# Expert stage of a transformer layer: pools that wait tile by tile, a new order of the left-hand pools, and another pace of the gate steps

## The chip, the cores and the metric

The kernel runs on one core of a Trainium2 chip. The metric is the device time of one execution in microseconds (us). Engines are named as in the profile: PE (TensorE; PEld its weight loads), DVE (VectorE), ACT (ScalarE), POOL (GpSimd, which issues the row gathers) and SP (SyncE, which issues nearly all direct DMA transfers). A queue name with a q, such as SPq, means DMA issues.

## The reference

One layer over 1024 tokens of width 1024: modulation, projections, windowed attention with a context of 256 tokens, a short convolution, a merge, and then an expert layer (PEER) whose 16384 experts are single rows of two tables. The expert layer is what this document is about:

```python
def peer(h, w_q, sub_keys, u_tab, v_tab):          # per chunk t of 128 tokens
    qh = (t @ w_q).reshape(T, 8, 2, 128)
    s = jnp.einsum('thpd,hpnd->thpn', qh, sub_keys)         # 128 scores per head and half
    s_top, i_top = lax.top_k(s, 16)
    cand = s_top[:, :, 0, :, None] + s_top[:, :, 1, None, :]
    best, pos = lax.top_k(cand.reshape(T, 8, 256), 16)      # 16 of 256 pairs
    idx = ...                                               # expert numbers, 128 per token
    g = jax.nn.softmax(best, axis=-1)
    act = jax.nn.gelu(jnp.einsum('thkd,td->thk', jnp.take(u_tab, idx, axis=0), t))
    return jnp.einsum('thk,thkd->td', g * act, jnp.take(v_tab, idx, axis=0))
```

The layer's result goes through a last rmsnorm.

## The kernel before

The tokens are two halves of 512. Up to about 1090 us the kernel does everything ahead of the experts; `stage2` of the second half ends with the scores of 16 key chunks, whose top values and their indices go to `sv` and `si`. The selection for the first half (`gates(0)`) runs beside it in the pool "gate0".

In the expert stage the first half is done densely: all 128 blocks of 128 experts are multiplied with all 512 tokens, and a gate matrix, zero for experts not chosen, weights the result. `slot_dense` (L1158) is one block i1. It loads the block of `v` (`v32`, 512 KB), and two slots ahead that of `u`, both in four shared buffers (tag uv32), splits each into two f16 parts (`uh` and `vh` on ACT, `ul` and `vl` on DVE), does 24 `ups` matmuls of 512 columns, a gelu on ACT into `gel`, the product of `gel` with the gates `gt` on DVE, and splits that into `wdh` (ACT) and `wdl` (DVE). Four slots make a group; in the four slots after it the group's eight outputs are done, two in a slot, each 4 x 3 matmuls of 512 columns (`res` for five of them, which stay in PSUM, and `vps` for three, which DVE adds into `part`). For the first three blocks `gel` comes from DRAM, where `early_u` put it; the weights of blocks 3 to 5 (`u_first`) are loaded and split through the pool "wts" before the stage, and that pool is then closed. The second half's tokens are done partly in that way, for 384 tokens (`slot_mix`, no `ups` of its own; its gates are built in the course of the first half), while for 128 tokens of it, and for the dot products of all 512, rows are gathered: `dots` gathers 4 x 128 rows of `u` (POOL) and multiplies each with the token on DVE; `rows_out` does so with `v`.

Gates come in steps. `select` picks the experts of 128 tokens (12 steps, nearly all on DVE; four of them hold the wide `eq` operations; it ends in `ci`, the row numbers that the gathers need). `build_g` spreads them into the gate matrix (20 steps: one-hot products `e`, `ah`, `al` on DVE, 16 `fbank` matmuls of 128 columns on PE, copies into `ge` on ACT, and after two steps a write of `ge` to DRAM (`gd`, 1 MB), from where `gt` is loaded). In the expert stage `ge` has one buffer and its write is issued from ACT's queue. `gates_stream` (L1043) orders selections 0, 1, 2, build 0, selection 3, build 1, build 2; a build waits for the dots of its tokens and yields False until they are done.

`run_side` (L1059) weaves this into the main loop. After each main step it takes as many row steps and gate steps as are due. The gate steps' due count `gdue` grows by 1 in each main step until selection 0 is done, then by GATES_D (L36) times what the main step spent on PE by a meter (columns / 2370); a step that yields False ends the inner loop and leaves `gdue` as it is. What is left when the main loop ends is done at once. The loop runs over 376 main steps (one in each of the first four slots, then three in a slot); row steps come at 478/361 for each. In order of the first half's slots, from slot 8 on (PIN_FROM, L47), PE, DVE and ACT keep the order in which the program was written; before that, and on SP and POOL throughout, a planner of the framework orders the work by its own estimate of when each instruction can start.

A pool is a stretch of SBUF (left-hand or right-hand stack) or of PSUM. Where a new pool takes the place of closed ones, its first tiles wait until everything in the closed pools that lie under it is released. `run` (L1408) closes "gate0", "x1", "s2", "half1", "wts" and two PSUM pools and then opens, one after the other, "psV" (PSUM), "acc" (left), "dense0" (left) and "gate1" (right, in `open_gate`, L1016). From the bottom, the left stack holds "const", and, in the closed part, "wts" (24 KB a partition: four weight tiles `whl`, two `w32`), "half1" (32 KB: `hT`, `cT`, `aT` of the second half) and "gate0".

Of the kernel before, what the change touches and what calls it, by code (L numbers as in the profile page):

```python
# [11 lines left out]
F16 = mybir.dt.float16  # L12
# [6 lines left out]
PSUM = bass.MemoryType.PSUM  # L19

D = 1024
# [10 lines left out]
NDENSE = 512  # L32
NMIX = 384
LATE_DOTS = 34
GATES_B = 0.64
GATES_D = 0.072  # L36
AHEAD = 1
GR = 8
GATE_AT = (2, 5)
# [3 lines left out]
SUB = 4  # L43
# [79 lines left out]
class K:  # L123
# [9 lines left out]
        self.waiting = []  # L133
        self.turned = None

    def pool(self, name, side=None, space=None, bufs=1):
        kw = {}
        if side is not None:
            kw["side"] = side
        if space is not None:  # L140
            kw["space"] = space
        g = self.tc.tile_pool(name=name, bufs=bufs, **kw)
        p = g.__enter__()
        return g, p
# [871 lines left out]
    def open_gate(self, name, side, ge_bufs):  # L1016
        nc, a = self.nc, self.a
        self.ge_bufs = ge_bufs
        g, self.pg = self.pool(name, side=side)
        p = self.pg  # L1020
        io32 = p.tile([128, 128], F32, name="io32", tag="dot", bufs=1)
        nc.sync.dma_start(io32, a["iota"])
        io16 = p.tile([128, 128], F16, name="iotas")
        nc.vector.tensor_copy(io16, io32)
        self.iota = io16.rearrange("p (a b) -> p a b", b=REP).unsqueeze(1).to_broadcast([128, TB, 128 // REP, REP])
        self.cand = p.tile([128, 8, NCAND], F32, name="cand", tag="cand", bufs=1)
        nc.vector.memset(self.cand[:, :, 16:128], NEG)
        self.iota16 = p.tile([128, 16, 16], F16, name="iota16")
        nc.vector.tensor_copy(self.iota16, io32[:, 0:16].unsqueeze(2).to_broadcast([128, 16, 16]))
        return g  # L1030
# [28 lines left out]
    def run_side(self, main, gates=None, grate=0.0, rows=None, rate=0.0, first=None):  # L1059


        pe, dve = self.nc.tensor, self.nc.vector
        last = pe.spent
        due = gdue = 0.0
        alive = gates is not None
        for _ in main:
            spent = pe.spent - last
            with nullcontext() if dve.pin else self.tc.issue_after(dve.last):
                due += rate
                while due >= 1.0:  # L1070
                    due -= 1.0
                    if next(rows, False) is False:
                        due = 0.0
                gdue += 1.0 if first is not None and first not in self.sel else grate * spent
                while alive and gdue >= 1.0:
                    r = next(gates, StopIteration)
                    alive = r is not StopIteration
                    if r is False:
                        break
                    gdue -= 1.0  # L1080
            last = pe.spent
        if alive:
            for _ in gates:
                pass
# [50 lines left out]
    def split_v(self, i1, v32, p):  # L1135
        if v32 is None:
            return self.vparts[i1]
        vh = p.tile([128, D], F16, name="vh", tag="vh", bufs=2 * SUB)
        vl = p.tile([128, D], F16, name="vl", tag="vl", bufs=2 * SUB)
        self.nc.scalar.activation(vh, v32, AF.Copy, scale=16.0)  # L1140
        self.late[0].append((vl, v32, 16.0, vh))
        if i1 >= 128 - 2 * SUB:
            self.vparts[i1] = vh, vl
        return vh, vl
# [13 lines left out]
    def slot_dense(self, i1, p, pv, outs):  # L1158
        nc = self.nc
        nb = NDENSE // 32  # L1160
        hh, hl = self.h2h[0], self.h2l[0]
        self.load_u(i1 + 2, p)
        v32 = self.load_v(0, i1, p)
        self.block_gates(0, i1, p)
        wh = self.pac.tile([128, NDENSE], F16, name="wdh", tag="wdh", bufs=2 * SUB)
        wl = p.tile([128, NDENSE], F16, name="wdl", tag="wdl", bufs=2 * SUB)
        ge = p.tile([128, NDENSE], F32, name="gel", tag="gel", bufs=2)
        if i1 < UPRE:
            nc.sync.dma_start(ge, self.ged[i1])
        else:  # L1170
            uh, ul = self.uparts.pop(i1)
            ps = pv.tile([128, 512], F32, name="ups", tag="v", bufs=3)
            for k in range(8):
                self.mm3(ps, uh[:, k, :], ul[:, k, :], hh[:, k, :], hl[:, k, :], k == 0, k == 7)
        self.lows(1)
        self.lows(0)
        if outs:
            yield 0
        if i1 >= UPRE:
            nc.scalar.activation(ge, ps, AF.Gelu, scale=2.0 ** -12)  # L1180
        self.split_u(i1 + 2, p)
        vh, vl = self.split_v(i1, v32, p)
        ends = []
        for k, out in enumerate(outs):
            ends.append(out())
            if k == 0:
                yield 0
        for end in ends:
            end()
        gev = ge.rearrange("p (b t) -> p b t", t=16)  # L1190
        for q in range(2):
            qs = slice(nb * q, nb * q + nb)
            nc.vector.tensor_mul(gev[:, qs, :], gev[:, qs, :], self.gts[q][:, :, i1 % GR, :])
        nc.scalar.activation(wh, ge, AF.Copy, scale=256.0)
        self.late[0].insert(0, (wl, ge, 256.0, wh))
        yield 0
        return vh, vl, wh, wl

    def slot_mix(self, i1, p, outs):
        nc = self.nc  # L1200
        nb = NMIX // 32
        v32 = self.load_v(1, i1, p)
        self.block_gates(1, i1, p)
        self.lows(0)
        vh, vl = self.split_v(i1, v32, p)
        wh = self.pac.tile([128, NMIX], F16, name="wdh", tag="wdh", bufs=2 * SUB)
        wl = p.tile([128, NMIX], F16, name="wdl", tag="wdl", bufs=2 * SUB)
        parts = [w.rearrange("p (b t) -> p b t", t=16) for w in (wh, wl)]
        for q in range(2):
            qs = slice(nb * q, nb * q + nb)  # L1210
            g = self.gts[q][:, :, i1 % GR, :]
            nc.scalar.activation(parts[0][:, qs, :], g, AF.Copy, scale=256.0)
            self.late[0].insert(q, (parts[1][:, qs, :], g, 256.0, parts[0][:, qs, :]))
        yield 1
        self.lows(0)
        for out in outs:
            out()()
            yield 1
        return vh, vl, wh, wl
# [166 lines left out]
    def experts(self, p, pv):  # L1386
# [4 lines left out]
        steps = 3 * 128 - 2 * SUB  # L1391
        self.run_side(islice(main, steps), self.gates_stream(), GATES_D, rows, (512 - LATE_DOTS) / (steps - 15.0), (1, 0))
        accs[0] = self.whole_acc("acc0")
# [14 lines left out]
    def run(self):  # L1408
# [9 lines left out]
        for hf in (1, 0):  # L1418
            g, p = self.pool(f"half{hf}", side="left")
# [39 lines left out]
        self.close(g_pw)  # L1459
        self.close(g_pa)  # L1460
        self.close(g_pf)
        g_pv, pv = self.pool("psV", space=PSUM)
        self.pf, self.ftag = pv, ("v", 3)
        self.bank = self.fbank
        g_ac, self.pac = self.pool("acc", side="left")
        self.part = self.pac.tile([128, 8 - NRES, HALF], F32, name="part")
        gd, pd = self.pool("dense0", side="left")
        g_g = self.open_gate("gate1", "right", 1)
        self.experts(pd, pv)
        self.close(gd)  # L1470
        self.close(g_ac)
        self.close(g_g)
        self.close(g_pv)
        self.close(self.g_pc)
# [63 lines left out]
```

## Time and profile before

| | |
|---|---|
| median of three runs | 3026.91 us (3026.48 to 3030.73) |
| the profiled execution | 3026.57 us, its span 3024.8 us |
| mean granted TensorE clock | 0.981 |
| PE, DVE, ACT, POOL busy | 95%, 88%, 39%, 35% |
| moved by DMA | 795.74 MB, 263 GB/s over the span |

The numbers of the stretches are times in us from the start of the span. A granted clock of 1.00 is 2.4 GHz, 0.50 is 1.2 GHz. The expert stage begins about 1075 (first `ups`), its first half ends about 2480, and its second half about 3010.

### The profile page before, as it was taken

Reading aid. Unit: us, or ns where it says so; the run is one execution under the profiler, and the core shown is the slowest. Engines: PE = TensorE matmul, PEld = TensorE weight load, DVE = VectorE, ACT = ScalarE, POOL = GpSimd, SP = SyncE. Lnnn points to the kernel's source line nnn. Section 1 sums busy time; section 2 is a strip of 40 time slices with the busy share of each in tenths; the row PEclk is TensorE's granted clock in tenths of the full one; section 3 lists DMA queues with packets and bytes.
Section 4 is the critical chain, followed back from the end, with each engine's and each line's share of the span. In section 5 each row is a group of like instructions: output and inputs, shape, how many; then the busy total and the mean of one; then the engine's idle time right before and its main releaser. Section 6 shows DMA issues by size and latency. Waiting matters only on the chain.

```text
span 3024.8 us, 49092 instructions
## 1 busy us (share of the span) xinstructions
PE 2869.4 (95%) x18685; PEld 1527.1 (50%) x18685; DVE 2647.7 (88%) x5438; ACT 1174.2 (39%) x1878; POOL 1063.1 (35%) x814
## 2 busy tenths in 40 slices
PE   6899999989989978999999999999999989999998
PEld 2465555444444433444444444444444446767675
DVE  7788776699999979999899998999979979888887
ACT  4844576423434232233233332333333323433342
POOL 3200012201121004554444444555444435455553
PEclk9999999999999988999999999999999999999999
DMA  6234436654445448899899998999989989999995
GB/s 225 94 116 123 117 125 183 227 169 151 177 167 192 160 154 287 321 334 321 307 321 345 341 345 292 328 328 333 342 318 334 325 294 316 381 366 351 349 365 197
DMA packets 327197, 795.74 MB, mean 263 GB/s; under 512 B 22960, under 2 KB 147248, under 8 KB 319792
## 3 DMA queue, kind: packets, MB, share of 16 engines
q1 hardware_dynamic: 219536, 372.08, 37.1%
q0 software_dynamic: 103968, 395.36, 35.4%
q10 hardware_dynamic: 3456, 25.17, 2.0%
q8 instruction: 146, 2.39, 0.3%
q14 instruction: 91, 0.75, 0.1%
HBM read 696.31 MB, written 96.21 MB: 262 GB/s over the span
## 4 chain that ended last, share of the span: by engine, by line
PE 44%; DVE 16%; issue 6%; POOL 3%; DMA 3%; ACT 1%; SPq 0%; DVEq 0%; POOLq 0%; ACTq 0%
PE res L72 23%; PE ups L72 13%; PE vps L72 5%; DVE row L72 3%; POOL row L917 3%; DMA row<-u,ci 2%; DVE vl L72 1%; PE fbank L72 1%; DVE e L72 1%; DVE eq L72 1%; PE bank L72 1%; DVE ul L72 1%; DVE si L72 1%; DVE wdl L72 1%; DVE sv L72 1%
## 5 line engine op out<-in xcount | busy, mean ns | idle before, releaser
L917 POOL DMA_INDIRECT row<-u,ci x512 | 674.6, 1318 | 899.5 <-DVE row L72 637.7
L72 DVE SCALAR_TENSOR_TENSOR row<-row,hn 128x1024 f32<-128x1024 f32 x512 | 614.6, 1223 | 75.5 <-DMA row<-u,ci 57.9
L72 PEld LDWEIGHTS <-vh 128*128 128x128 f16 x5120 | 469.6, 98 | 357.3 <-issue 24.3
L72 PE MATMUL res<-wdl,vh 128*128 128x128 f16 (+2 forms) x2176 | 628.2, 306 | 13.7 <-DVE wdl L72 13.6
L72 PE MATMUL res<-wdh,vh 128*128 128x128 f16 (+2 forms) x2176 | 625.6, 306 | 12.2 <-ACT wdh L72 12.2
L72 PE MATMUL res<-wdh,vl 128*128 128x128 f16 (+2 forms) x2176 | 625.3, 306 | 4.7 <-DVE vl L72 4.7
L72 PE MATMUL ups<-h,uh 128*128 128x512 f16 x1952 | 582.4, 380 | 0.0
L72 PEld LDWEIGHTS <-whl 128*128 128x128 f16 x3288 | 317.5, 100 | 370.8 <-issue 50.0
L72 PE MATMUL bank<-hT,whl 128*128 128x512 f16 x1584 | 378.7, 388 | 15.4 <-ACT hT L72 6.0
L72 ACT ACTIVATE vh<-v 128x1024 f16<-128x1024 f32 x248 | 260.1, 1049 | 307.1 <-PE res L72 163.0
L72 PE MATMUL ups<-h,ul 128*128 128x512 f16 x976 | 371.3, 380 | 5.6 <-DVE ul L72 5.6
L72 PEld LDWEIGHTS <-vl 128*128 128x128 f16 x2560 | 250.8, 98 | 195.8 <-DVE vl L72 22.9
L72 DVE SCALAR_TENSOR_TENSOR vl<-v,vh 128x1024 f16<-128x1024 f32 x248 | 301.9, 1218 | 10.3 <-ACT vh L72 10.3
L72 PEld LDWEIGHTS <-uh 128*128 128x128 f16 x1952 | 190.9, 98 | 228.7 <-issue 1.9
L917 POOL DMA_INDIRECT row<-v,ci x128 | 217.3, 1698 | 173.6 <-DVE wdl L72 88.6
L72 ACT ACTIVATE gel<-ups 128x512 f32<-128x512 f32 x125 | 74.6, 597 | 403.1 <-PE ups L72 392.2
L72 ACT ACTIVATE wdh<-gel 128x512 f16<-128x512 f32 x128 | 80.5, 629 | 354.1 <-DVE gel L72 338.0
L72 ACT ACTIVATE ge<-fbank 128x512 f32<-128x512 f32 x224 | 121.6, 594 | 222.3 <-PE fbank L72 187.0
L72 DVE SCALAR_TENSOR_TENSOR racc<-row,fig,racc 128x1024 f32<-128x1024 f32 x127 | 162.6, 1281 | 9.3 <-DMA row<-v,ci 7.0
L72 DVE TENSOR_TENSOR e<-iotas,ii 128x1024 f16<-128x1024 f16 x224 | 153.3, 708 | 7.9 <-ACT ii L72 4.8
L72 PEld LDWEIGHTS <-ul 128*128 128x128 f16 x976 | 95.6, 98 | 122.4 <-DVE ul L72 7.0
L72 PE MATMUL vps<-wdh,vh 128*128 128x512 f16 x384 | 145.6, 379 | 5.2 <-ACT ge L72 4.3
(223 smaller groups left out, 4211.4 us busy)
## 6 DMA issues: line engine op xcount, KB each, us to landing
v<-v SPq DMA_DIRECT2D x248, 512.0 KB
u<-u_t SPq DMA_DIRECT2D x122, 512.0 KB
gd<-ge POOLq DMA_DIRECT2D x32, 1024.0 KB
gt<-gd SPq DMA_DIRECT2D x32, 1024.0 KB
wm<-w_mod SPq DMA_DIRECT2D x48, 512.0 KB
gd<-ge ACTq DMA_DIRECT2D x24, 1024.0 KB
gt<-gd SPq DMA_DIRECT2D x32, 768.0 KB
w<-w_in SPq DMA_DIRECT2D x34, 512.0 KB
```

The source lines that it names most:

```text
L72: r = f(*args, **kw)
L917: self.nc.gpsimd.indirect_dma_start(out=r, out_offset=None, in_=tab, in_offset=bass.IndirectOffsetOnAxis(ap=ci[:, s:s + 1], axis=0))
```

## The change

Five pools, "psV", "acc", "dense0", "gate0" and "gate1" (the last two through `open_gate`), are opened with `reuse_waits="tile"`: a new tile then waits for what lay under that tile alone. A sixth pool of this kind, "parts", is opened on the left below "acc"; the tiles `vh`, `vl` and `wdl` move from "dense0" into it (8 buffers of 2, 2 and 1 KB a partition, 40 KB), so that "acc" (`part`, `wdh`; 14 KB) and the rest of "dense0" (`v32`/`u32`, `gt`, `gel`, `uh`, `ul`) lie 40 KB higher. GATES_D goes from 0.072 to 0.085, and where the gate stream yields False, `gdue` is cut to at most 1.

```diff
-GATES_D = 0.072
+GATES_D = 0.085
@@ pool
-    def pool(self, name, side=None, space=None, bufs=1):
-        kw = {}
+    def pool(self, name, side=None, space=None, bufs=1, **kw):
@@ open_gate
-        g, self.pg = self.pool(name, side=side)
+        g, self.pg = self.pool(name, side=side, reuse_waits="tile")
@@ run_side
                     if r is False:
+                        gdue = min(gdue, 1.0)
                         break
@@ split_v
-        vh = p.tile([128, D], F16, name="vh", tag="vh", bufs=2 * SUB)
-        vl = p.tile([128, D], F16, name="vl", tag="vl", bufs=2 * SUB)
+        vh = self.ppt.tile([128, D], F16, name="vh", tag="vh", bufs=2 * SUB)
+        vl = self.ppt.tile([128, D], F16, name="vl", tag="vl", bufs=2 * SUB)
@@ slot_dense (and slot_mix with NMIX)
-        wl = p.tile([128, NDENSE], F16, name="wdl", tag="wdl", bufs=2 * SUB)
+        wl = self.ppt.tile([128, NDENSE], F16, name="wdl", tag="wdl", bufs=2 * SUB)
@@ run
-        g_pv, pv = self.pool("psV", space=PSUM)
+        g_pv, pv = self.pool("psV", space=PSUM, reuse_waits="tile")
-        g_ac, self.pac = self.pool("acc", side="left")
+        g_pt, self.ppt = self.pool("parts", side="left", reuse_waits="tile")
+        g_ac, self.pac = self.pool("acc", side="left", reuse_waits="tile")
-        gd, pd = self.pool("dense0", side="left")
+        gd, pd = self.pool("dense0", side="left", reuse_waits="tile")
         self.close(g_ac)
+        self.close(g_pt)
```

## Rows read from the trace of the kernel before

**Rows 1.** The page's first part: engine, busy us (share of span), instructions.

```profile
PE 2869.4 (95%) x18685; PEld 1527.1 (50%) x18685; DVE 2647.7 (88%) x5438; ACT 1174.2 (39%) x1878; POOL 1063.1 (35%) x814
```

**Rows 2.** Chain of waits in order of time: start, us, engine, tile, count.

```profile
1543.39 2.59 PE res L72 x12
...
1549.47 5.18 PE ups L72 x24
```

**Rows 3.** Stretches: length; busy PE, PEld, DVE, ACT, POOL; clock; DMA share; GB/s.

```profile
1028.00:1062.00 34.00, 33.25 (x209) 17.15 (x207) 34.00 (x206) 8.00 (x13) 0.00 (x0) 1.00 0.29 94
1062.00:1092.40 30.40, 27.00 (x143) 12.63 (x141) 23.39 (x136) 4.65 (x7) 0.00 (x0) 0.94 0.13 37
1092.40:1104.40 12.00, 0.05 (x2) 0.11 (x2) 2.71 (x9) 1.74 (x3) 0.00 (x0) 0.63 0.97 315
1104.40:1148.00 43.60, 37.12 (x152) 15.34 (x152) 43.60 (x146) 19.87 (x25) 0.55 (x1) 0.89 0.55 180
1148.00:1170.00 22.00, 15.02 (x53) 5.83 (x52) 15.09 (x35) 3.75 (x5) 10.62 (x11) 0.72 1.03 371
```

**Rows 4.** Timeline of SP's DMA issues: start, us, queue, line, transfer.

```profile
1028.25 24.65 SPq L170 DMA_DIRECT2D whl<-ws_wq  x6
1062.01 0.33 SPq L173 DMA_DIRECT2D w<-u_t  x1
...
1092.47 0.33 SPq L1132 DMA_DIRECT2D v<-v  x1
```

**Rows 5.** What SP's queue waited for, 1060 to 1210: us, times, longest.

```profile
SPq L1022 <- DVE si L72: 21.8, 1, 21.8
...
SPq L1132 <- PE ups L72: 7.0, 1, 7.0
```

**Rows 6.** Timeline of POOL, 1000 to 1100: its only instruction.

```profile
1004.93 0.53 POOL L1009 DMA_DIRECT2D gd<-ge  x1 [7.04 <-ACT ge L72]
```

**Rows 7.** Timeline of DVE at the start; in brackets idle before, and releaser.

```profile
1097.26 1.22 DVE L72 SCALAR_TENSOR_TENSOR vl<-v,vh 128x1024 f16<-128x1024 f32 x1 [10.32 <-ACT vh L72]
1102.92 0.76 DVE L72 TENSOR_TENSOR gel<-gel,gt 128x256 f32<-128x256 f32 x2 [4.44 <-DMA gel<-ged]
...
1146.18 0.29 DVE L72 SCALAR_TENSOR_TENSOR ci<-fig 128x128 int32<-128x128 f32 x1
```

**Rows 8.** Stretches with selections, then with a build; columns as in rows 3.

```profile
1180.00:1490.00 310.00, 304.93 (x1403) 137.10 (x1401) 298.35 (x578) 96.77 (x123) 156.53 (x117) 0.99 0.89 317
1512.00:1775.00 263.00, 261.81 (x1402) 126.49 (x1401) 247.87 (x395) 93.35 (x130) 124.39 (x96) 1.00 0.94 337
```

**Rows 9.** Timeline of DVE: one `eq` step, and a slot without a step.

```profile
1404.38 0.68 DVE L72 TENSOR_TENSOR eq<-iota,ab 128x1024 f16<-128x1024 f16 x1
...
1407.54 1.22 DVE L72 SCALAR_TENSOR_TENSOR row<-row,hn 128x1024 f32<-128x1024 f32 x1
...
1562.23 1.22 DVE L72 SCALAR_TENSOR_TENSOR ul<-u,uh 128x1024 f16<-128x1024 f32 x1
...
1571.01 1.21 DVE L72 SCALAR_TENSOR_TENSOR ul<-u,uh 128x1024 f16<-128x1024 f32 x1
```

**Rows 10.** What PE waited for, 1175 to 2455: us, times, longest.

```profile
PE res L72 <- DVE wdl L72: 6.2, 3, 2.9
...
PE res L72 <- DVE vl L72: 3.3, 5, 0.8
```

**Rows 11.** Stretches at the end of the first half; columns as in rows 3.

```profile
2462.90:2478.50 15.60, 7.68 (x82) 6.58 (x81) 11.36 (x18) 4.84 (x10) 1.04 (x1) 0.76 0.65 221
...
2482.00:2999.00 517.00, 515.96 (x4606) 356.85 (x4604) 432.63 (x607) 197.65 (x395) 270.11 (x170) 1.00 0.94 341
```

**Rows 12.** Timeline of ACT at the end of the first half.

```profile
2470.34 2.29 ACT L72 ACTIVATE ge<-fbank 128x512 f32<-128x512 f32 x4 [5.70 <-DMA gd<-ge]
```

More of the change, by code (lines that the diff above doesn't have):

```diff
@@ L1206, in slot_mix @@
         wh = self.pac.tile([128, NMIX], F16, name="wdh", tag="wdh", bufs=2 * SUB)
-        wl = p.tile([128, NMIX], F16, name="wdl", tag="wdl", bufs=2 * SUB)
+        wl = self.ppt.tile([128, NMIX], F16, name="wdl", tag="wdl", bufs=2 * SUB)
         parts = [w.rearrange("p (b t) -> p b t", t=16) for w in (wh, wl)]
```

## Prediction, made before the changed kernel was built

> **What bounds the kernel now.** The page's first part is read first: TensorE (PE) is busy for 95% of the span and DVE for 88% [rows 1]. A share that high says only that a gain must come from time in which PE stands still or runs at its lower clock. The chain of waits in order of time shows the steady state of the expert stage: 24 `ups` matmuls in 5.18 us and each output of 12 matmuls in 2.59 us [rows 2], so 0.216 us a matmul of 512 columns, and a slot of one `ups` and two outputs is 5.18 + 2 x 2.59 = 10.36 us. Then the table of stretches shows where that rate is missed, and there are two places: the start of the stage [rows 3] and the end of its first half [rows 11]. From 2482 to 2999 PE is busy for 516 of 517 us [rows 11], and the diff touches nothing there but where tiles lie.
>
> At the start PE is idle for all of 1092.4 to 1104.4, then has 152 matmuls in 43.6 us and 53 in 22 us, at granted clocks of 0.89 and 0.72 [rows 3]. Together 207 matmuls in 77.6 us; at 0.216 us they need 44.7 us, so 33 us are lost. Why: SP issues the last weight load at 1062.01 and the first `v` load only at 1092.47, with 30 us between in which its queue moves little (DMA share 0.13) [rows 3, 4]. The waits of SP's queue name what held it: the last `si` of the scores for the iota load, and the last `ups` matmul for the first `v` [rows 5]. These are releases of whole pools: `ups` reads weights of the closed pool "wts", and nothing in `v32` needs them. The data were there long before, since POOL issued its last `gd` write of the first gates at 1004.93 [rows 6].
>
> **Part 1: waits tile by tile, and the new layout.** It removes the wait of the first `v`, `gt` and `gel` loads for 1092.4. Their tiles (pool "dense0") now lie behind "parts" (40 KB a partition) and "acc" (14 KB), which takes them off the 24 KB of "wts" and onto "half1" and "gate0"; the former was last read in the projections of stage 2, the latter's work ended about 1005. What still overlies the weights that `ups` reads is `vh` and `wdl`, written by ACT and DVE. So the loads can run in the idle 30 us. What is late next is DVE, not PE: it is full in 1028 to 1062 and in 1104.4 to 1148 [rows 3], and the first row gather hangs on it (`ci` at 1146.18) [rows 7]. Between the scores and that, DVE stands idle for 10.32 us before the first `vl` and 4.44 us before the first `gel` [rows 7], 14.8 us. These are the gain, because what follows up to `ci` is DVE work without holes. PE's 12 us come with it and aren't added. Bounds: 0 (DVE finds another wait) to 28 us (also most of the two later holes; of the 33 us lost, some 5 stay: DVE idles for 6.9 of the 22 us from 1148 on [rows 3], when the first gathers arrive). I take **15 us**, the 14.8 of the two rows.
>
> Costs of the move: the early transfers (`v` of 512 KB, `gt` of 1 MB) go through SP ahead of nothing that is due, as the weight loads end at 1062.01 [rows 4]; covered by the idle queue. If that cover is gone (the planner, which orders the work before slot 8, places them earlier) they pass the six `whl` loads that SP issues from 1028.25 on [rows 4]; see the last rival. "gate0" is opened tile by tile too; its first load feeds only setup, and I cost it at nothing, with 2 us either way. In the pools' waits themselves nothing is added that I can see; 0 to 2 us.
>
> The Trainium skill (DMA: Bandwidth & Descriptors, section "Issuing engines are not separate DMA queues") says that transfers of all issuing engines run on the same 16 DMA engines and interleave, which speaks against early loads beside weight loads. By it the gain would shrink by what the weights lose. The trace's shares of 0.29 and 0.13 before 1092.4 [rows 3] leave room, so I take nothing off.
>
> **Part 2: the pace of the gate steps.** The counts come from the code. The first half has 376 main steps; a slot is worth 48 x 512/2370 = 10.37 in the meter's units. Gate steps: 4 selections of 12 and 3 builds of 20, 108 in all; 12 go one by one at the start. At 0.072 a slot earns 0.747 of a step: 12 + 0.747 x 122 = 103, and **5 build steps are left over** for the drain behind the loop. At 0.085 it earns 0.881, enough for all, less what is lost while the stream waits for dots (the cap now forfeits the arrears). Counting the yields through, selections 1 and 2 end at slot 33 (before 37), build 0 runs in slots 39 to 61 (before 39 to 64), build 1 in 76 to 97 (before 82 to 107), build 2 from slot 105, when its dots are done, to main step 373 of 376. Nothing is left, by a margin of one slot.
>
> *Removed:* the drain. PE's 82 matmuls of 128 columns between 2462.9 and 2478.5 take 15.6 us [rows 11]; at a quarter of 0.216 us each, 0.054, they need 4.4 us. The rest is waiting: ACT holds for the `gd` write before it (5.70 us, and a second time) since `ge` has one buffer [rows 12]. In the slots a write has two slots until the next, and is hidden. The 4.4 us of matmuls only move. So 11 us, and 1 us behind it at low clock: **12 us**, bounds 8 (one or two steps left over, 2.2 us each) to 13.
>
> *Added:* 0.134 step more per slot while steps run. DVE pays. A slot without a step takes DVE 8.78 us (from `ul` to `ul`) [rows 9]. In 1180 to 1490, selections running, DVE is busy 298 of 310 us [rows 8]; these are (310 - 5)/10.36 = 29.4 slots, so 10.15 us each, 1.37 us of it steps, or 1.83 us a step. At the new pace: 10.15 + 0.134 x 1.83 = 10.40 us against PE's 10.36. In the builds (1512 to 1775) DVE is busy 248 of 263 us, 94% [rows 8]; a step has 16 matmuls, a slot there is 10.36 + 0.747 x 16 x 0.054 = 11.01 us, DVE's part 10.38, a step (10.38 - 8.78)/0.747 = 2.1 us, and the new pace gives 10.66 against PE's 11.12: still PE. So the selections now just fill DVE, and what PE pays is at runs of heavy steps: an `eq` step takes 3.16 us [rows 9], its slot 1.6 us more than PE's, and with three steps in four slots the free fourth gives it back; with seven in eight it doesn't. PE's waits for `wdl` and `vl` between 1175 and 2455 are 9.5 us now [rows 10]. I take **2 us more**; bounds 0 and 9 (as much again).
>
> After such waits the granted clock falls: over the drain its mean is 0.76 of full speed, over 1148 to 1170 0.72 [rows 3, 11], between the levels of 2.4 and 1.2 GHz. The Trainium skill (TensorE: Matmul & The Clock Gate, section "HAM oscillation — how this bites in real kernels") has the same against many gaps: each is paid twice. In 1180 to 1490 the clock is 0.99 with 5 us idle [rows 8], so here it is under 1 us per wait, and inside my 2.
>
> **Sum.** Against the profiled execution (3026.57 us, 1.8 us over its span, and 0.3 us under the median of the three runs): 3026.6 - 15 - 12 + 2 = **3001.6 us**, with 2993 to 3010 for this case alone.
>
> **Rivals.** *Only the drain goes* (the loads stay behind a release, or DVE meets a wait on "parts"): 3026.6 - 12 + 2 = 3016.6. For it: `vh` still overlies weights read until 1092.4. Against: the `gel` products, which the selection hangs on, don't. *The start gives nearly all*: if DVE's early lead also covers the waits after 1140, -28: 2988.6. *DVE takes over*: if the denser steps cost PE all the excess (36 selection steps at half of 1.6 us = 29 us) and the start still gives 15: 3026.6 - 15 - 12 + 29 = 3028.6, no change; against it, DVE's 94% in the builds and the free slots 33 to 39 and 97 to 105. *Slower: SP stands.* An early load placed ahead of the last weight loads waits in SP's queue for a reader of "gate0", and the six `whl` loads behind it come late. PE holds up to four weights, so it decides from some 20 us of standing; each us beyond goes onto the span, and above 25 more it ends slower: at 60 us of standing 3026.6 - 25 + 40 = 3041.6. Against: the gates end about 1005 and the last loads come later [rows 4, 6].
>
> **Chances.** Forecast 0.62, drain only 0.14, start in full 0.07, DVE takes over 0.08, SP stands 0.09. The range takes in the forecast, drain only and part of the third: 2990 to 3019. A measurement of this kernel can tell about 0.2%, 6 us: faster 0.82, same 0.08, slower 0.10.
>
> **What would show it.** Right: `v`, `gt` and `gel` issued before 1090 and `ci` near 1131; no PE hole of 12 us before the first `res`; no `ge` wait for `gd` behind the last slot, and the step to the second half some 27 us before 2480; PE's waits for `wdl` and `vl` at 10 to 13 us, before slot 33 and 74. Wrong: `ci` still at 1146, five steps left, DVE full through 1500 with PE waiting at each group, or weights late around 1040.

## The result, and the profile of the changed kernel

The changed kernel takes 2997.65 us (median; 2995.85 to 3004.6) against 3026.69 us of the kernel before, a ratio of 0.9911 with a 95% interval of 0.9897 to 0.9925: 29 us faster by the two medians, 27 us by the ratio. The prediction was 3001.6 us. The profiled execution took 2997.38 us, its span is 2995.6 us, its mean granted clock 0.987.

The page's first part (engine, busy us, share of the span, instructions; before: [rows 1]):

```profile
PE 2858.1 (95%) x18685; PEld 1521.8 (51%) x18685; DVE 2647.2 (88%) x5438; ACT 1176.0 (39%) x1878; POOL 1052.4 (35%) x814
```

The shares are those of before, and the same instructions ran: the gain is time in which PE stood or ran slowly. Where it lay is seen in the timeline of SP's DMA issues (start, us, queue, line, transfer), against [rows 4]:

```profile
1000.24 0.50 SPq L1132 DMA_DIRECT2D v<-v  x1
1001.10 0.78 SPq L1092 DMA_DIRECT2D gt<-gd  x1
...
1017.10 0.50 SPq L1169 DMA_DIRECT2D gel<-ged  x1
...
1035.56 12.02 SPq L169 DMA_DIRECT2D whl<-ws_wq  x3
1059.04 0.33 SPq L172 DMA_DIRECT2D w<-u_t  x1
1059.42 0.42 SPq L1021 DMA_DIRECT2D io<-iota  x1
```

The first `v` load is issued at 1000.24 instead of 1092.47, between the weight loads, and the last weight load still goes out, at 1059.04 (before at 1062.01; that difference is taken apart below). The stretches at the start, one with selections, and two at the end of the first half (length; busy PE, PEld, DVE, ACT, POOL; clock; DMA share; GB/s), against [rows 3, 8, 11]:

```profile
1028.00:1062.00 34.00, 34.00 (x212) 17.61 (x211) 33.18 (x198) 9.76 (x16) 0.00 (x0) 1.00 0.48 157
1062.00:1092.40 30.40, 24.54 (x117) 11.29 (x116) 25.99 (x142) 6.62 (x9) 0.00 (x0) 0.89 0.07 25
1092.40:1104.40 12.00, 11.27 (x50) 4.58 (x51) 12.00 (x51) 5.78 (x8) 0.00 (x0) 1.00 0.43 144
1104.40:1148.00 43.60, 31.61 (x127) 12.77 (x126) 36.39 (x88) 13.80 (x17) 7.66 (x8) 0.85 0.60 199
1148.00:1170.00 22.00, 22.00 (x95) 9.61 (x94) 22.00 (x60) 6.24 (x8) 10.75 (x9) 0.92 0.91 328
1180.00:1490.00 310.00, 302.14 (x1394) 135.81 (x1393) 290.02 (x559) 97.16 (x124) 149.36 (x114) 1.00 0.91 318
2434.00:2449.60 15.60, 15.36 (x84) 7.38 (x82) 12.07 (x21) 4.67 (x8) 8.18 (x7) 1.00 0.89 303
2465.00:2972.00 507.00, 505.25 (x4560) 352.47 (x4559) 430.39 (x604) 196.82 (x389) 263.39 (x170) 1.00 0.95 343
```

PE's hole of 12 us before 1104.4 is gone (11.27 of 12.00 busy). In 1104.4 to 1148, though, PE now stands 12.0 us instead of 6.5, above all for one `wdl` that DVE makes behind its first row products (timeline of PE, in brackets the wait before):

```profile
1145.27 0.58 PE L72 MATMUL res<-wdl,vh 128*128 128x512 f16 x1 [6.38 <-DVE wdl L72]
```

Over 1062 to 1170 PE's idle time falls from 28.8 to 18.6 us. In the same stretch DVE's idle time falls from 7.0 + 9.3 + 0 + 6.9 = 23.2 us [rows 3] to 4.4 + 0 + 7.2 + 0 = 11.6 us. What stays is the wait for the first row gathers. On DVE (start, us, operation; in brackets idle before, and releaser), against [rows 7]:

```profile
1129.80 0.28 DVE L72 SCALAR_TENSOR_TENSOR ci<-fig 128x128 int32<-128x128 f32 x1
...
1136.96 1.23 DVE L72 SCALAR_TENSOR_TENSOR row<-row,hn 128x1024 f32<-128x1024 f32 x1 [4.47 <-issue]
...
1140.70 1.23 DVE L72 SCALAR_TENSOR_TENSOR row<-row,hn 128x1024 f32<-128x1024 f32 x1 [2.51 <-DMA row<-u,ci]
```

`ci` comes at 1129.80 instead of 1146.18; the 4.47 and 2.51 us behind it are the remaining hole. For the first of them the profile names no releaser; POOL issued that row's gather at 1131.10. What PE waited for from 1175 to 2455 (us, times, longest), against [rows 10]:

```profile
PE res L72 <- DVE wdl L72: 6.4, 4, 2.1
PE res L72 <- DVE vl L72: 4.3, 6, 0.8
```

10.7 us in ten waits instead of 9.5 in eight, the longest 2.1 instead of 2.9. A second execution of the changed kernel has 9.2 us in thirteen, so this sum tells no difference. And ACT at the end of the first half, against [rows 12]:

```profile
2443.79 1.09 ACT L72 ACTIVATE ge<-fbank 128x512 f32<-128x512 f32 x2 [6.01 <-PE fbank L72]
2444.91 0.33 ACTq L72 DMA_DIRECT2D gd<-ge  x1
```

The last build step lies inside the last slot, and no `ge` waits for a `gd` write: the drain is gone.

**Splitting the difference.** Two events are in every kernel: SP's last `u_t` load into `w`, the last load ahead of the expert stage, and the second half's first narrow `res` matmul (384 columns). The stretch between them, called S below, holds what the change touches, but for one cost just ahead of it. From the timeline of PE, first the kernel before, then the changed one:

```profile
2500.40 0.33 PE L72 MATMUL res<-wdh,vh 128*128 128x384 f16 x1
```

```profile
2470.34 0.33 PE L72 MATMUL res<-wdh,vh 128*128 128x384 f16 x1
```

S is 2500.40 - 1062.01 = 1438.4 us before and 2470.34 - 1059.04 = 1411.3 us after: 27.1 us. Of the 29.2 us between the two spans another 3.0 lie ahead of the last `u_t` load (1062.01 against 1059.04), and the rest of the span is 0.9 us longer.

The 3.0 us are a cost and a larger scatter. The two kernels run in step up to the last of the eight `h2d` writes (a result of stage 2) that SP issues; first the kernel before, then the changed one:

```profile
1022.01 0.37 SPq L813 DMA_DIRECT2D h2d<-hn  x1
```

```profile
1016.69 0.36 SPq L812 DMA_DIRECT2D h2d<-hn  x1
```

From there to the last `u_t` load it is 40.0 us before and 42.35 after; in all runs below it is 40.0 where the first `v` load comes late and 42.3 to 42.4 where it comes early. The `u_t` load waits for DVE (`sv`), and in the changed kernel DVE does four `gel` products ahead of it, for which the early loads have brought the data, and stands 0.8 us behind them:

```profile
1039.64 0.41 DVE L72 TENSOR_TENSOR gel<-gel,gt 128x256 f32<-128x256 f32 x1
...
1044.66 1.08 DVE L72 TENSOR_TENSOR gel<-gel,gt 128x256 f32<-128x256 f32 x3
```

So the early loads cost 2.3 us ahead of S, and from the `h2d` write on the change gains 27.1 - 2.3 = 24.8 us. The `h2d` write itself came 5.3 us earlier; that is scatter between executions, for over the runs below it lies between 1014.7 and 1022.5, whenever `v` is loaded.

Within S, `ci` comes 1146.18 - 1062.01 = 84.2 us behind the load before and 70.8 after, 13.4 us less; with the 2.3 us taken off, **11.1 us are the start** (up to 12.6 in the runs below whose start is the same, where `ci` comes 69.3 to 70.8 behind the load); the other 13.7 are the first half and its end. Where these lie shows at the first `ups` matmul of the last `u` block, before and after:

```profile
2451.65 0.60 PE L72 MATMUL ups<-h,uh 128*128 128x512 f16 x2
```

```profile
2437.97 0.59 PE L72 MATMUL ups<-h,uh 128*128 128x512 f16 x2
```

From there to the narrow `res` it is 48.8 us before and 32.4 after. Of these 16.4 us 4.3 are not gained: by then the changed kernel has done five build steps more, 80 matmuls at the prediction's 0.054 us. So **12.1 us are the drain**, and 1.6 lie between.

### The profile page after: what moved, and what is told of

Read it like the earlier page. It is cut to its first block, busy times and chain, and to the rows that moved or that the text cites. A ratio compares the mean times of both kernels' runs of the same rounds, so it can differ in the third digit from the quotient of the medians.

```text
span 2995.6 us, 49091 instructions
## 1 busy us (share of the span) xinstructions
PE 2858.1 (95%) x18685; PEld 1521.8 (51%) x18685; DVE 2647.2 (88%) x5438; ACT 1176.0 (39%) x1878; POOL 1052.4 (35%) x814
## 4 chain that ended last, share of the span: by engine, by line
PE 44%; DVE 10%; DMA 4%; issue 3%; POOL 2%; ACT 0%; SPq 0%; DVEq 0%; POOLq 0%; ACTq 0%
PE res L72 23%; PE ups L72 13%; PE vps L72 5%; DVE row L72 4%; DMA row<-u,ci 2%; POOL row L916 2%; PE fbank L72 1%; DVE vl L72 1%; DMA v<-v 1%; DVE ul L72 1%; DVE eq L72 1%; DVE wdl L72 1%; DVE gel L72 0%; DVE part L72 0%; ACT ge L72 0%
## 5 line engine op out<-in xcount | busy, mean ns | idle before, releaser
L72 PEld LDWEIGHTS <-vh 128*128 128x128 f16 x5120 | 468.4, 98 | 341.4 <-issue 12.5
L916 POOL DMA_INDIRECT row<-v,ci x128 | 210.9, 1648 | 179.6 <-DVE wdl L72 90.0
L72 DVE SCALAR_TENSOR_TENSOR racc<-row,fig,racc 128x1024 f32<-128x1024 f32 x127 | 162.5, 1280 | 10.7 <-DMA row<-v,ci 9.7
```

The costliest lines, as they stand in the source:

```text
L72: r = f(*args, **kw)
L916: self.nc.gpsimd.indirect_dma_start(out=r, out_offset=None, in_=tab, in_offset=bass.IndirectOffsetOnAxis(ap=ci[:, s:s + 1], axis=0))
```

## The experiments

The theory: the start's gain comes from the early loads and is limited by DVE's chain to `ci`; the end's gain is the drain, removed by the pace; the two add; denser steps cost DVE, and so PE, a little. The times of all runs (ratio to the kernel before on the same chip, with its 95% interval; S from the profiled execution; its last column is the time from the last `u_t` load to `ci`). In both of the last columns the 2.3 us have to be taken off the gain of a kernel whose first `v` load comes early, that is of all but the kernel before, the pace alone and the old layout:

| kernel | median, us | ratio | S, us | to `ci`, us |
|---|---|---|---|---|
| before | 3026.69 | 1 | 1438.4 | 84.2 |
| changed | 2997.65 | 0.9911 (0.9897 to 0.9925) | 1411.3 | 70.8 |
| changed, once more | 3001.95 | 0.9916 (0.9902 to 0.9929) | 1410.0 | 70.8 |
| loads and layout alone | 3009.44 | 0.9949 (0.9935 to 0.9963) | 1425.7 | 69.5 |
| pace alone | 3016.12 | 0.9966 (0.9952 to 0.9979) | 1429.9 | 84.4 |
| tile by tile, old layout | 3001.72 | 0.9915 (0.9902 to 0.9928) | 1417.9 | 73.8 |
| whole pools, new layout | 3002.49 | 0.9926 (0.9913 to 0.9939) | 1413.6 | 71.2 |
| no cut of the arrears | 3036.80 | 1.0040 (1.0026 to 1.0055) | 1447.5 | 69.4 |
| more DVE work at the start | 3003.19 | 0.9920 (0.9908 to 0.9933) | 1420.8 | 73.3 |
| early row gathers | 3010.30 | 0.9947 (0.9932 to 0.9961) | 1424.0 | 70.7 |
| row rate 482 | 3012.15 | 0.9958 (0.9944 to 0.9971) | 1420.9 | 70.8 |
| row rate 474 | 3002.91 | 0.9929 (0.9916 to 0.9943) | 1410.8 | 69.3 |
| pace 0.12 | 3029.71 | 1.0020 (1.0010 to 1.0030) | 1442.4 | 69.8 |
| even pace | 3003.22 | 0.9921 (0.9908 to 0.9935) | 1416.9 | 70.8 |

**How far one execution tells.** No edit: the changed kernel again.

> The changed kernel once more, beside the two others and the kernel before on one chip, to see how far a second execution of the same program lies from the first: the time from the last `u_t` load to the second half's first narrow output (1411.3 us in the first profile) and the median (2997.65 us). Theory (differences of 2 to 5 us between the variants are their programs' own): within 1.5 us of 1411.3 in that stretch. Rival (executions of one program differ as much as the variants do in that stretch): 3 to 8 us apart, and gains of that size in single profiles mean nothing.

S came out at 1410.0, 1.3 us from the first; the last `u_t` load at 1064.82, 5.8 us from the first. So S tells differences of a few us where spans and medians do not, as far as one pair of executions can say, while the last `u_t` load scatters more: over the profiles here it lies between 1055.4 and 1064.8, with and without the early loads. Differences of that size come and go within S. The clearest place is 770 us into it, where PE waits for a `wdl` (2.1 us in the first execution, 0.8 in the second) and the granted clock differs over the 30 us (columns as in rows 3):

```profile
1829.04:1859.04 30.00, 27.12 (x119) 11.78 (x118) 26.38 (x47) 6.95 (x10) 13.32 (x10) 0.94 1.00 349
```

```profile
1834.82:1864.82 30.00, 28.43 (x132) 12.66 (x131) 25.45 (x46) 8.94 (x13) 12.91 (x10) 1.00 0.98 339
```

The theory of this run held.

**The parts one at a time.** Pools and layout with the old pace:

```diff
-GATES_D = 0.085
+GATES_D = 0.072
...
-                        gdue = min(gdue, 1.0)
```

> The changed kernel with the old pace (0.072, no cut of the arrears): pools and layout alone. Theory (the two parts are separate: 16 us come at the start, the rest is the drain): `ci` near 1130 instead of 1146, the first half's slots some 16 us earlier, but five build steps are again left over and the drain of about 15.6 us with its `ge` waits is back: 3026.7 - 16 = 3011, between 3008 and 3013. Rival (the pace carries the gain, because denser steps also let the gates be ready sooner): 3020 or more. Rival (the loads are everything, and the drain is hidden by something else once the start is earlier): 3000 or less.

3009.44 us; `ci` 69.5 us behind the last `u_t` load. The drain is back where it was. The stretch of it, and ACT in it:

```profile
2445.50:2461.00 15.50, 8.98 (x85) 7.11 (x84) 12.84 (x20) 6.06 (x11) 1.15 (x1) 0.68 0.69 239
```

```profile
2452.40 2.29 ACT L72 ACTIVATE ge<-fbank 128x512 f32<-128x512 f32 x4 [4.97 <-DMA gd<-ge]
...
2458.66 2.29 ACT L72 ACTIVATE ge<-fbank 128x512 f32<-128x512 f32 x4 [3.97 <-DMA gd<-ge]
```

Five steps again, some 15.5 us, a clock of 0.68, and the two `gd` waits: an earlier start does nothing for the drain. Then the kernel before with the new pace alone:

```diff
-GATES_D = 0.072
+GATES_D = 0.085
...
+                        gdue = min(gdue, 1.0)
```

> The kernel before with the new pace (0.085 and the cut of the arrears) and nothing else. Theory: the start is as before (`ci` near 1146, PE idle 12 us before 1104), no build step is left behind the last slot, the second half starts some 11 to 12 us earlier, and the denser steps cost nothing that can be seen: 3026.7 - 12 = 3014.7, between 3012 and 3018. Rival (denser steps cost DVE and so PE 9 us, and in the changed kernel only the early start hid that): 3023 to 3026. Together with the run of the loads alone the gains should add up to the 29 us of the whole change within 3 us.

3016.12 us, no drain, the start as before. By the ratios the parts give 1 - 0.9949 and 1 - 0.9966, 15.4 and 10.3 us, together 25.7 against 26.9 for the whole; the intervals (4 us either way) hold that. By S, with the 2.3 us taken off, they give 10.4 and 8.5, 18.9 against 24.8 and 26.1. So the two parts are separate and add as far as the ratios can tell. The 6 to 7 us by which S is short in single executions do not lie in the drain: from the first `ups` of the last block on, the pace saves 16.4 us beside the old start and 16.3 beside the new one. Up to there it costs 7.8 us beside the old start, and 1.9 or nothing beside the new one (first and second execution of the changed kernel); in each 4.3 us are the moved matmuls. Why denser steps are dearer behind the late start stays open.

**What makes the loads early.** The new layout and the waits tile by tile came in one edit. First the waits without the layout (`vh`, `vl`, `wdl` back in "dense0", no "parts"):

```diff
-        vh = self.ppt.tile([128, D], F16, name="vh", tag="vh", bufs=2 * SUB)
+        vh = p.tile([128, D], F16, name="vh", tag="vh", bufs=2 * SUB)
...
-        g_pt, self.ppt = self.pool("parts", side="left", reuse_waits="tile")
```

> The changed kernel with `vh`, `vl` and `wdl` back in "dense0" and no pool "parts", so all tiles lie as before; the waits stay tile by tile and the pace stays new. The first `v32` buffer and `wdh` now lie over weights that `ups` reads until about 1076 to 1092. Theory (DVE is what is late at the start, and it needs `gel`, `gt` early, not `v`): the first `v` load comes late again, but the `gel` products and with them the selection start early: `ci` at 1130 to 1136, time 2998 to 3006. Rival (the layout is needed, since any load that stands at the head of SP's queue holds all behind it): `ci` at 1143 or later, time 3010 to 3016.

3001.72 us. The first `v` load waited again for the last `ups` on its weights, 12.5 us in SP's queue, and went out at 1077.46, 19 us behind the last `u_t` load where the kernel before took 30. From the timeline of SP, and from its waits (us, times, longest):

```profile
1077.46 0.33 SPq L1132 DMA_DIRECT2D v<-v  x1
1078.09 2.91 SPq L1092 DMA_DIRECT2D gt<-gd  x2
1081.05 4.27 SPq L1169 DMA_DIRECT2D gel<-ged  x1
```

```profile
SPq L1132 <- PE ups L72: 12.5, 1, 12.5
```

`ci` still came 10.4 us earlier than before. Both numbers of the theory held, its reason only in part: `gt` and `gel` did not overtake the late `v`, they came right behind it in SP's queue. What helped is that `v` waited for what lay under its own tile alone and so went out 11.5 us sooner. Then the layout without the waits:

```diff
-        g_pt, self.ppt = self.pool("parts", side="left", reuse_waits="tile")
+        g_pt, self.ppt = self.pool("parts", side="left")
...
-        gd, pd = self.pool("dense0", side="left", reuse_waits="tile")
+        gd, pd = self.pool("dense0", side="left")
```

and likewise for "psV", "acc" and the gates' pools.

> The changed kernel with its layout ("parts" and all) and pace, but every pool waits as a whole again, as before. Theory (at the start the tile-wise wait is the cause and the layout by itself gives nothing): the first `v` is issued behind the last `ups` matmul again, from the last `u_t` load to `ci` it takes 84 us as before (71 in the changed kernel), and only the pace's gain is left: 3013 to 3018, as in the run of the pace alone. Rival (the layout matters also with waits of whole pools, because "dense0" then lies over pools that closed early): 71 to 75 us to `ci`, 2997 to 3005.

3002.49 us and 71.2 us to `ci`: my theory fell, its rival held. SP's timeline shows why:

```profile
1004.25 0.33 SPq L1132 DMA_DIRECT2D v<-v  x1
1004.63 0.43 SPq L1092 DMA_DIRECT2D gt<-gd  x1
...
1081.32 0.33 SPq L1021 DMA_DIRECT2D io<-iota  x1
```

With "parts" below it, all of "dense0" lies over pools whose last use was long past, so even a wait for whole pools ends at 1004. What still waits for the last scores is the iota load of "gate1", at 1081.32 instead of 1059.42, and that costs no more than the 2.3 to 3.6 us by which S is longer. Up to `ci`, with the 2.3 us taken off where they apply, tile waits alone give 10.4 us, the layout alone 10.6 and both 11.1 to 12.6. In S, against the pace alone (1429.9), they give 12.0, 14.0 and 16.3 to 17.6; some 2 to 3 us of what either lacks alone arise in the place 770 us into S at which the two executions of the changed kernel differ too (in these runs a `wdl` wait of 2.9 us and a clock of 0.89 over the 30 us). **Either part brings most of it; they take away the same wait twice.**

**Is DVE what is late at the start?** The memset of the candidates (0.81 us) is done 8 times at the opening of "gate1":

```diff
-        nc.vector.memset(self.cand[:, :, 16:128], NEG)
+        for _ in range(8 if name == "gate1" else 1):
+            nc.vector.memset(self.cand[:, :, 16:128], NEG)
```

> The changed kernel with the memset of the selection's candidates done 8 times instead of once at the opening of the second half's gates: 5.7 us more work on DVE (0.81 us each) between the scores and the first selection, nothing on PE. Theory (after the change DVE is what is late at the start, so its work stands on the path): from the last `u_t` load to `ci` some 5 to 6 us more (76 to 77), the first half 4 to 6 us later, 3002 to 3004. Rival (what the change gave back is PE's 12 us hole before the first outputs, and DVE has slack there): `ci` moves, but the end of the first half moves by less than 2 us, 2997 to 2999.

`ci` came 2.6 us later for 5.7 us of work, not the 5 to 6 expected, so DVE had some 3 us of slack up to there. S grew by 9.5 us against the first and 10.8 against the second execution of the changed kernel, the median by only 5.5 and 1.2. DVE's work at the start is paid in the direction the theory says; the size stays open.

**Filling the hole at the first gathers.** Four gathers go out four row steps ahead of the first product, and the row steps' rate goes from 478 to 482 over 361 main steps:

```diff
+        early = []
+        if t == 0:
+            early = [self.row(self.a["u"], ci, s) for s in range(4)]
+            for _ in range(4):
+                yield
         for s in range(128):
-            r = self.row(self.a["u"], ci, s)
+            r = early.pop(0) if early else self.row(self.a["u"], ci, s)
...
-... rows, (512 - LATE_DOTS) / (steps - 15.0), (1, 0))
+... rows, (516 - LATE_DOTS) / (steps - 15.0), (1, 0))
```

> The changed kernel with the first four row gathers of the first token group issued four row steps ahead of their first product on DVE (the row steps' rate goes from 478 to 482 over the same steps, so that the later groups come when they did). DVE stands for 7.2 us at the first gathers now, and PE waits 6.4 us for a `wdl` in that stretch. Theory (DVE on the path, so filling its hole is a gain): the hole goes, 2991 to 2994, 4 to 7 us faster than the changed kernel. Rival (PE is late there for another reason, the weights `ul` and the slots' own chain): the hole goes and the time stays within 2 us, 2996 to 2999.

Slower than the changed kernel by 12.7 and 8.4 us by the medians of its two sets of runs, by 12.7 and 14.0 by S; neither theory had that. To tell the halves of the edit apart, the rate alone:

```diff
-... rows, (512 - LATE_DOTS) / (steps - 15.0), (1, 0))
+... rows, (516 - LATE_DOTS) / (steps - 15.0), (1, 0))
```

> The changed kernel with the row steps' rate at 482 instead of 478 over the same steps and no early gathers: half of the edit of the run with early rows, which came out 12.7 us slower than the changed kernel. Theory (the first half is so close to DVE's limit that DVE's added and shifted work there is paid, four more row steps of about 1.2 us each among it): 3002 to 3011, most of the 12.7 us again. Rival (the rate is harmless, and the early gathers themselves cost it, because the four products that follow come closer together behind the hole and wait for their rows): 2996 to 3001.

3012.15 us, S 9.6 to 10.9 us longer: the cause is the rate, by itself. The early gathers on top of it show neither gain nor loss: S is 3.1 us longer with them, the ratio 0.9947 instead of 0.9958. They did take away PE's idle time at the start, as the stretch shows that is 1104.4 to 1148 in the changed kernel, counted from the last `u_t` load (PE 38.55 us busy instead of 31.61):

```profile
1102.90:1146.50 43.60, 38.55 (x166) 16.48 (x165) 38.36 (x100) 15.35 (x20) 9.48 (x7) 0.92 0.60 204
```

but in the 315 us from 1175 on PE is busy 299.8 us instead of 307.1, and the gain is lost again. What PE waited for in the run of the rate alone, 1175 to 2500:

```profile
PE res L72 <- DVE wdl L72: 7.7, 5, 2.6
PE res L72 <- DVE vl L72: 7.0, 10, 0.8
```

14.7 us instead of 10.7 and 9.2. Over all of S, first in the changed kernel, then here (columns as in rows 3):

```profile
1059.04:2470.34 1411.30, 1377.69 (x6909) 644.03 (x6906) 1307.11 (x2461) 467.35 (x637) 634.28 (x482) 0.99 0.89 315
```

```profile
1062.63:2483.55 1420.92, 1380.94 (x6908) 644.43 (x6906) 1313.48 (x2471) 466.71 (x637) 640.27 (x487) 0.99 0.89 315
```

PE stands 40.0 us instead of 33.6 and is busy 3.3 us longer with the same matmuls. So 0.8% more row steps, under 0.05 us a slot, cost 10 us. And fewer (474):

```diff
-... rows, (512 - LATE_DOTS) / (steps - 15.0), (1, 0))
+... rows, (508 - LATE_DOTS) / (steps - 15.0), (1, 0))
```

> The changed kernel with the row steps' rate at 474 instead of 478 (482 was 10 us slower). By the counts of the code one slot in eleven then has three row steps instead of four, which leaves DVE some 1.2 us there, no gate step is left behind the last slot, and four row steps move into the second half. Theory (in the first half DVE's work is paid, in both directions): PE's waits for `wdl` and `vl` behind 1175 fall to 5 to 8 us, the stretch from the last `u_t` load to the second half's first narrow output falls from 1411 to 1403 to 1408, 2990 to 2995. Rival (any shift of the row steps against the slots costs, in whatever direction, because the changed kernel's phase happens to fit): 1413 to 1422, 3000 to 3010.

S is 1410.8, that of the changed kernel: less DVE work in the first half gains nothing there, and this shift by itself costs nothing, so both expectations fell. Three rates look like a knee just where the changed kernel stands. That the shift to 482 costs by the place of its steps in the slots, and not by their work, is not excluded: the even pace below loses 6 us with no more work. The median is 3002.91 all the same, because the second half took 533.3 us instead of 525.3. PE's timeline at its end (in brackets the wait before):

```profile
2970.14 1.11 PE L72 MATMUL fbank<-id,racc 128*128 128x128 f32 x4 [2.99 <-DVE racc L72]
```

Four row products more than the second half's rate has room for stand behind its last steps, PE waits for them, and the clock falls behind that (0.83 from 2967.8 to 2987.8): the drain of the first half in small, at the other end. Of the 8.0 us the wait is 3.0 and the clock some 2.8 (0.17 of 16.7 us of work); the rest is not itemised.

**The cut of the arrears.**

```diff
                     if r is False:
-                        gdue = min(gdue, 1.0)
                         break
```

> The changed kernel without the cut of the arrears (pace 0.085 kept). By the counts of the code the arrears that gather while the stream waits for dots come out as bursts: 6 build steps in slot 39, 3 in slot 72, 12 in slot 105, and the stream is done at main step 339 of 376. Theory (a burst is DVE work that PE can't cover: a build step costs DVE 2.1 to 2.5 us, a slot leaves DVE some 1.6 us): twelve steps are 25 to 30 us of DVE work in one slot of 10.4 us, of which PE's stock of finished weights covers some 10; PE waits for `ul` or `vl` 10 to 20 us about slot 105 and 2 to 6 us about slot 39: 3009 to 3024, that is 12 to 25 us slower than the changed kernel. Rival (the weights made ahead and the free slots behind take it up): 2998 to 3001, the cut is worth nothing.

3036.80 us, slower than the kernel before: the cut is worth 35 to 39 us, more than the 12 to 25 expected. The burst of 12 steps (columns as in rows 3; the clock is 1.00 in the 10 us ahead of it and behind it):

```profile
2210.00:2250.00 40.00, 23.82 (x166) 17.35 (x164) 33.04 (x53) 13.97 (x22) 4.95 (x4) 0.62 0.47 176
```

and PE's waits from 2200 to 2310:

```profile
PE fbank L72 <- DVE e L72: 6.0, 2, 5.2
PE fbank L72 <- ACT ge L72: 4.2, 2, 3.5
PE fbank L72 <- DVE part L72: 3.4, 1, 3.4
PE fbank L72 <- DVE al L72: 2.7, 1, 2.7
```

In 40 us PE does 23.8 us of work at a clock of 0.62: 16 us idle and up to 9 us lost to the clock. The burst of six steps in slot 39 adds one wait of 7.7 us for `e`. My estimate had let PE's finished weights cover 10 us, but the `fbank` matmuls stand in PE's own order, so PE waits there for each step's one-hots, and the estimate had left the clock out. The Trainium skill (TensorE: Matmul & The Clock Gate, section "HAM oscillation — how this bites in real kernels") says that gaps are paid a second time in matmuls at the lower clock; the trace agrees, with a second payment of up to 9 us on 16.

**A denser pace.**

```diff
-GATES_D = 0.085
+GATES_D = 0.12
```

> The changed kernel with the pace at 0.12 instead of 0.085: 1.24 gate steps in a slot instead of 0.88. By the costs in the prediction a slot of a selection then takes DVE 8.78 + 1.24 x 1.83 = 11.06 us against PE's 10.36, and a slot of a build 8.78 + 1.24 x 2.1 = 11.4 against PE's 10.36 + 1.24 x 0.86 = 11.4. Theory (DVE is the limit of a denser pace in the selections, so the pace has an optimum just where DVE is full): 36 selection steps in 29 slots lose 0.7 us each, 20 us; with free slots behind them giving some back, 3008 to 3020. Rival (PE's stock of finished weights and the free slots cover it all): within 3 us of the changed kernel.

3029.71 us: S 31 us longer, where 10 to 22 were expected. PE's waits, 1175 to 2500:

```profile
PE res L72 <- DVE wdl L72: 17.0, 6, 4.7
PE vps L72 <- ACT ge L72: 9.2, 19, 2.2
```

The direction is that of the theory (DVE limits it in the selections), the size half as much again: builds lose too, by waits for `ge` (9.2 us here, 3.6 in the changed kernel). And a pace evened out, 0.076 until the dots of the third group are done, 0.09 from there:

```diff
-GATES_D = 0.085
+GATES_D = 0.076
+LAST_D = 0.09
...
+                gdue += 1.0 if first is not None and first not in self.sel else (LAST_D if first and 2 in self.ndots else grate) * spent
```

> The changed kernel with a pace of 0.076 until the dots of the third token group are done and 0.09 from there on, instead of 0.085 throughout. By the counts of the code nothing is left behind the last slot, and the selections and builds 0 and 1 spread over the slots that stood free of steps (in the changed kernel 33 to 39, 97 to 105, 12 of 128). Theory (a denser pace costs PE its waits for DVE in the selections, and the old pace avoids part of them): PE's waits for `wdl` and `vl` behind 1175 fall from 10.7 to 6 to 8 us, 2992 to 2996. Rival (the free slots already give back what the dense ones take, and the place of the heavy steps against the slots' own DVE work decides): within 2.5 us of the changed kernel, 2995 to 3000.

3003.22 us, ratio 0.9921, S 5.6 to 6.9 us longer. The theory fell: PE's waits for `wdl` and `vl` stayed (7.3 and 5.1). The rival's 2995 to 3000 was missed too. In S PE stands 2.4 us longer and is busy 3.3 us longer than in the changed kernel; why is open. By its median none of the variants beat the changed kernel.

## Why the prediction was right, point by point

*Start, 15 us: 11.1 to 12.6 measured to `ci`, 10.4 in S for the loads alone (the 2.3 us ahead of S taken off both).* The chain was the one named: DVE's idle time ahead of `ci` went, PE's 12 us came with it and weren't added. But the size was 2 to 4 us too large. `ci` was forecast near 1131 and came at 1129.80; 5.3 us of that are the earlier arrival at the stage, so that closeness is luck. Two steps of this part were incomplete. I took tile waits and layout for one cause; the runs show two, each nearly enough up to `ci`. And I costed the move at nothing on DVE: the early `gel` and `gt` let DVE do four `gel` products ahead of the last scores, all that follows on DVE comes 2.3 us later, and PE's wait for `qql` grows by as much. From PE's timeline, before and then after:

```profile
1073.72 0.23 PE L72 MATMUL bank<-whl,qql 128*128 128x128 f16 x1 [2.65 <-DVE qql L72]
```

```profile
1070.74 0.29 PE L72 MATMUL bank<-whl,qql 128*128 128x128 f16 x1 [4.99 <-DVE qql L72]
```

It is 5.0 in every kernel with `v` issued about 1000 and 2.6 where it comes late. That 2.3 us is just over what I had bounded with 0 to 2 us, for another reason.

*Drain, 12 us: removed whole, 12.1 measured.* No step is left behind the last slot, as counted through; with the old pace five are, and they take 15.5 us again.

*Denser steps, +2 us: neither size nor sign is shown.* Up to the first `ups` of the last block, the moved matmuls taken off, the pace costs 3.5 us beside the old start; beside the new one the two executions of the changed kernel are 2.5 and 4.4 us ahead of the loads alone. PE's waits for `wdl` and `vl` were forecast to rise from 9.5 to 10 to 13 us, and came to 10.7 and 9.2. PE idles 7.9 and 6.1 us in 1180 to 1490 instead of 5.1 [rows 8], at a clock of 1.00 instead of 0.99, which over 310 us can give all of it back.

*The sum.* 25 us were forecast; from the `h2d` write on 24.8 and 26.1 us are seen in the two executions, in the medians 29.0 and 24.3. The mechanisms are those of the prediction, but the start is 2 to 4 us short and the 2 us for denser steps are not seen, so that the sum fits this well is in part luck.

*The rivals.* The slower one is refuted: the early loads go out between the `whl` loads, and the last of these has been issued 30.9 us behind the `h2d` write in both kernels. That the drain alone would go is refuted by `ci`. The full gain at the start did not come: the first gathers' hole stayed, and where the early gathers took PE's part of it away, the selections behind took the gain back. "DVE takes over" did not happen at 0.085, yet it was nearer than a chance of 0.08 says: a row rate 0.8% higher takes 10 us of the gain, and a pace of 0.12 all of it.

## What to carry to other kernels

Where a load waits for a closed pool, look first at which pools it lies over: laying it over something long finished did here what a finer wait does, and either was most of the gain. Work that is woven into a main loop should be counted to its last step, at the end of each half: five steps left over cost 12 us, and four row products at the other end up to 8 us; arrears that build up while the stream waits must be dropped, since paid out in a burst they cost 35 us or more. Before DVE is loaded further, change its rate by one per cent in both directions: here less gained nothing in that half and more cost 10 us, as at a knee, and a gain that fills a hole can be lost behind it, as that of the early gathers was. And where a gain is measured between two events of a trace, see that the change leaves the first of them in its place: here it had moved by 2.3 us.

## What the runs showed that I had not expected

Two executions of one program agree within 1.3 us over 1410 us of the expert stage, but their arrival at that stage differs by 5.8 us (1059.04 and 1064.82), so in this pair the scatter of the whole comes from ahead of it. And a loss this large: 0.8% more row steps in the first half, some 5 us of DVE work in all, cost 10 us of PE time, of which 6.4 us are idle time and 3.3 us longer busy time for the same matmuls.
